# Spreading the group norm's factors over the partitions: a DRAM round trip replaced by products with the identity

## The chip, the core and the metric

The kernel runs on one core of a Trainium2 chip. TensorE multiplies matrices, VectorE, ScalarE and GpSimd work elementwise, SyncE issues transfers. On-chip data lie in 128 partitions (SBUF, and PSUM for the results of TensorE). The metric is device time in microseconds (us) of one execution, smaller is better.

## The reference

One inference step of a one-layer decoder, for 512 prompt tokens and 8 sample tokens, all in fp32. The part that matters here is the retention branch: 4 heads, 256 key and 512 value dimensions, each head with a root-mean-square group norm over its 512 values per token:

```python
o_r, s_new = retention(qr, kr, vr, s0, chunk)
o_r = o_r * lax.rsqrt(jnp.mean(o_r * o_r, axis=-1, keepdims=True) + EPS)
o_r = o_r.reshape(B, T, RET_V) * ret_gn_g.astype(f32) * jax.nn.silu(g_r.astype(f32))
branch_a = o_r.astype(xn.dtype) @ w_pa
```

Before it stand an RMS norm and one large input projection; beside it a dilated-window attention branch; behind it gates, an output projection and a SwiGLU feed forward.

## The kernel before

Activations are kept transposed, features on the partitions and the 520 tokens along the row, as two halves of 260 (256 prompt and 4 sample tokens). All weights are one stream of 194 tiles of 128x1024. Each tile is loaded by SyncE (`load_sub`), its high part is made by ScalarE and its low part by VectorE (`split_sub`, L153 and L157), two tiles ahead of use. `unit` is one 128-row block of a projection: 8 K-steps of 6 matmuls each (`product`, L189), into one of two PSUM product banks (`pm`), then an evacuation on VectorE or ScalarE.

All other work of TensorE is slipped between those K-steps. It is written as Python generators on two tracks, P and S. `pump` is called after each K-step and takes one step of one track; during retention P and S take turns, so a P step comes every second K-step. `drain` and `finish` take the remaining steps of a track at once, with no product between. `later(n, fn)` puts an operation n pumps further on. The order so written is the order of instructions on each engine; every engine takes its own instructions in order and waits for the others by semaphores.

For each of the four heads `h`: four units of q and k with the rotation (`rot`), four of v (`ev_v`, L621 and L622, which copies the sample tokens' values to `vs`), four of the gate (`ev_g`). On track P run `gen_scores`, `gen_vT` and then `gen_out`; on track S runs `gen_sample`, the recurrence of the sample tokens with its own small norm (L563 to L580; `os` is its row of results, and L570 its product of squares). A new head's `gen_out` is pushed after the old one has been finished by force. After the last head come six units of gates (`gate`, L659), then `drain()`, then the attention part, whose projections are evacuated by ScalarE (L849, L851) and VectorE (`sT`, L853).

`gen_out` computes the head's outputs into `GT` (16 tiles, four a head) and their squares' sum `acc` over four tiles. It then sums over the partitions with TensorE: 4 products with a column of ones (L468) give `sp`, 128 partitions by 4 columns, so token 128 j + p stands on partition p in column j. `rstd_rows` makes the factors `r` of them: one VectorE operation (L219) and a power on GpSimd (L221). To multiply `GT`, whose partitions are features, each factor is needed on all partitions as a row `rs` of 512 tokens. The kernel gets it by a store of `r` to the DRAM tile `rd[h]` (L473) and a load of it that is broadcast over the partitions (L474), both on SyncE's queue. Four yields later it multiplies: per tile one VectorE operation (L479), a yield, one GpSimd operation with the gate (L481), a yield.

`bcast_cols` (L224 to L228) is there already for the first and the second norm: for each column j a product whose weight is the column `r[:, j]` repeated 128 times and whose moving operand is the identity, so that every output partition holds the column as a row. Side results stand in PSUM banks from `sbank`, three in rotation.

Of the kernel before, what the change touches and what calls it, by code (L numbers as in the profile page):

```python
# [8 lines left out]
F32 = mybir.dt.float32  # L9
F32R = mybir.dt.float32r  # L10
AF = mybir.ActivationFunctionType
# [6 lines left out]
T, NS, C, D = 512, 8, 520, 1024  # L18
HF, HT = 260, 256
RH, DK, DV = 4, 256, 512  # L20
# [8 lines left out]
def tile_hybrid_layer(  # L29
# [9 lines left out]
    V, A, G_, PE, SP = nc.vector, nc.scalar, nc.gpsimd, nc.tensor, nc.sync  # L39
# [4 lines left out]
    dpool = ctx.enter_context(tc.tile_pool(name="dpool", bufs=1, space=DRAM))  # L44
# [4 lines left out]
    def open_pool(name, side):  # L49
        return tc.alloc_tile_pool(name=name, bufs=1, side=side, reuse_waits="tile")  # L50

# [1 line left out]
    def halves(ap):  # L53
        return ap.rearrange("p (f c) -> p f c", f=2)

    def tokv(ap):
        return halves(ap)[:, :, :HT]
# [7 lines left out]
    def f32(ap):  # L65
        return ap.bitcast(F32)

# [1 line left out]
    rp = open_pool("rp", "right")  # L69
    vec = cpool.tile([128, 40], F32, name="vec")  # L70
    warm = cpool.tile([128, 1], F32, name="warm")
# [14 lines left out]
    mhalf = cst[:, 273:274]  # L86
    g1v, g2v, gfv, gnv = vec[:, 0:8], vec[:, 8:16], vec[:, 16:24], vec[:, 24:40]

# [1 line left out]
    tracks = {"P": deque(), "S": deque()}  # L90
    pattern = ["P"]
    tick = [0]
# [2 lines left out]
    def later(n, fn):  # L95
        delayed.append([n, fn])
# [37 lines left out]
            run_delayed()  # L134
            step(name)

# [1 line left out]
    raw, split = {}, {}  # L138

    NRAW = 4  # L140
# [64 lines left out]
    def sbank(name="sp"):  # L205
        return pside.tile([128, 512], F32, tag="s", name=name)
# [7 lines left out]
    BL = 65  # L214

    def rstd_rows(pool, ssq, rows, ncol, n, tag):
        """(ssq / n + eps) ** -0.5 of the [rows, ncol] sums in ssq"""
        v = pool.tile([128, 8], F32, tag=tag + "v", bufs=2, name="v")
        V.tensor_scalar(v[:rows, :ncol], ssq, 1.0 / n, EPS, op0=ALU.mult, op1=ALU.add)  # L219
        r = pool.tile([128, 8], F32, tag=tag + "r", bufs=2, name="r")  # L220
        G_.tensor_tensor(r[:rows, :ncol], v[:rows, :ncol], mhalf[:rows].to_broadcast([rows, ncol]), op=ALU.pow)  # L221
        return r

    def bcast_cols(out, r, rows, ncol):  # L224
        """out[:, j, :rows] = r[:, j] as a row, on all partitions"""
        for j in range(ncol):
            PE.matmul(out[:, j, :], r[:rows, j:j + 1].to_broadcast([rows, 128]), ident[:rows, :rows],
                      start=True, stop=True)  # L228

# [1 line left out]
    X0 = bpool.tile([128, 16, C], F32R, tag="bg", name="X0")  # L231
    X = bpool.tile([128, 16, C], F32R, tag="bx", name="X")

    def tmp(name="t"):
        return rp.tile([128, C], F32, tag="t", bufs=6, name=name)

    sp = sbank("warmup")
# [92 lines left out]
    def xsrc(k):  # L330
        return X[:, k, :], X[:, 8 + k, :]

    # ================= retention =================
    SCO = (0, 512, 896, 1152)
    scs = [rp.tile([128, 1408], F32R, name=f"sc{i}") for i in range(2)]
    for i in range(2):
        G_.memset(f32(scs[i][:, 1152:1280]), 0.0)
    rd = [dpool.tile([1, T], F32, name=f"rd{h}") for h in range(RH)]
    vd = [dpool.tile([8, DV], F32, name=f"vd{h}") for h in range(RH)]

    for h in range(RH):
# [91 lines left out]
        def gen_out(h, tens):  # L433
            v, kt = tens["v"], tens["kt"]
            three = ((0, 0), (0, 1), (1, 0))
            acc = rp.tile([128, T], F32, tag="rs", name="ssa")
            for c in range(4):
                sp = sbank()
                for jb in range(4):
                    i0 = min(jb * 128, HT)  # L440
                    for x, y in three:
                        PE.matmul(sp[:, i0:], v[x][:, jb, c * 128:(c + 1) * 128], scs[y][:, SCO[jb]:SCO[jb] + T - i0],  # L442
                                  start=jb == 0 and x == y, stop=jb == 3 and x == 1)
                    if jb == 0:
                        yield
                yield
                A.activation(tokv(GT[:, 4 * h + c, :]), halves(sp), AF.Copy)
                if c == 0:
                    A.activation(acc, sp, AF.Square)
                else:  # L450
                    sq = tmp("sq")
                    A.activation(sq[:, :T], sp, AF.Square)
                    later(2, lambda sq=sq: G_.tensor_tensor(acc, acc, sq[:, :T], op=ALU.add))
            for dt in range(2):
                sp = sbank()
                for jb in range(4):
                    for x, y in three:
                        PE.matmul(sp, kt[x][:, jb, dt * 128:(dt + 1) * 128], v[y][:, jb, :], start=jb == 0 and x == y,  # L458
                                  stop=jb == 3 and x == 1)
                    if jb % 2:  # L460
                        yield
                sf = tmp("sf")
                A.activation(sf[:, :DV], sp, AF.Copy)
                yield
                later(2, lambda sf=sf, dt=dt: SP.dma_start(s_p[0, 0, h, dt * 128:(dt + 1) * 128, :], sf[:, :DV]))
            sp = sbank()
            for j in range(4):
                PE.matmul(sp[:, j:j + 1], acc[:, j * 128:(j + 1) * 128], ones1, start=True, stop=True)  # L468
            yield
            r = rstd_rows(rp, sp[:, :4], 128, 4, DV, "gn")  # L470
            rs = rp.tile([128, T], F32, tag="rs", name="rs")
            yield
            SP.dma_start(rd[h].rearrange("o (j p) -> p (o j)", p=128), r[:, :4])  # L473
            SP.dma_start(rs, rd[h].to_broadcast([128, T]))  # L474
            for _ in range(4):
                yield
            for c in range(4):
                o = tokv(GT[:, 4 * h + c, :])
                V.scalar_tensor_tensor(o, o, gnv[:, 4 * h + c:4 * h + c + 1], halves(rs), op0=ALU.mult, op1=ALU.mult)  # L479
                yield  # L480
                G_.tensor_tensor(o, o, tokv(tens["g"][:, c, :]), op=ALU.mult)  # L481
                yield
# [146 lines left out]
        if h == 0:  # L629
            GT = bpool.tile([128, 16, C], F32, tag="bg", name="GT")  # L630
        go = push("P", gen_out(h, tens))
        if h:
            finish("S", gs)
# [8 lines left out]
            unit(8, xsrc, ev_g)  # L642


    # ================= gates of the first half =================
    sgp = [None, None]
    SG = {}
    GC = ((0, 1, 2), (3, 4, 5, 6, 7))
# [1 line left out]
    def open_gates(i):  # L650
        sgp[i] = open_pool(f"sg{i}", "left")
        n = len(GC[i])
        t = sgp[i].tile([128, 2 * n, C], F32, name=f"SG{i}")
        for j, c in enumerate(GC[i]):
            SG[0, c], SG[1, c] = t[:, j, :], t[:, n + j, :]
# [11 lines left out]
    drain()  # L667
    rp.release()

    # ================= attention =================  # L670
    olp = open_pool("olp", "left")
    OT = olp.tile([128, 2, AH, C], F32R, name="OT")
    sT = olp.tile([128, 3, 3, 128], F32, name="sT")
# [188 lines left out]
    for g in range(3):  # L862
        push("S", gen_srow(g))

    # ================= gates of the second half =================
    open_gates(1)
    todo = [(c, w) for c in GC[1] for w in range(2)]
    for c, w in todo[:-2]:
# [19 lines left out]
        gate(c, w)  # L888
    drain()

    # ================= sample attention =================
    def gen_satt(sa):
        Pm = sa.tile([128, 3, 1024], F32, name="Pm")
        G_.memset(Pm, 0.0)
# [95 lines left out]
            V.tensor_tensor(OT[:, 1, :, f * HF + HT:(f + 1) * HF], sv[:, :, 4 * f:4 * f + 4], f32(hi), op=ALU.subtract)  # L990
        yield

    # ================= merge =================
    GB = bpool.tile([128, 16, C], F32R, tag="bx", name="GB")
    for k in range(8, 16):
        gsplit(k, GB, 2 * k - 16)
# [22 lines left out]
    olp.release()  # L1019
    sgp[0].release()  # L1020

    # ================= output projection, residual, second norm =================
    hp = open_pool("hp", "left")
    hT = hp.tile([128, 8, C], F32, name="hT")
    rs2 = hp.tile([128, C], F32, name="rs2")
# [32 lines left out]
    def gen_norm2():  # L1058
        for _ in range(8):
            yield  # L1060
        sp = sbank()
        for j in range(8):
            PE.matmul(sp[:BL, j:j + 1], acc2[:, BL * j:BL * j + BL], ones1, start=True, stop=True)
        yield
        r = rstd_rows(fp, sp[:BL, :8], BL, 8, D, "n2")
        yield
        yield
        yield
        for f in range(2):
            sp = sbank()  # L1070
            bcast_cols(sp[:, :HF].rearrange("p (j c) -> p j c", c=BL), r[:, 4 * f:4 * f + 4], BL, 4)
            V.tensor_copy(rs2[:, f * HF:(f + 1) * HF], sp[:, :HF])
            yield

    # ================= feed forward =================
    pattern[:] = ["P"]
    push("P", gen_norm2())
    U = [None] * (2 * NFF)
# [34 lines left out]
    def fin_T(c, f):  # L1113
        h = hT[:, c, :]
        sp, sp2 = sbank(), sbank()
        for j in range(2):
            o = f * HF + 128 * j
            pe_T(sp[:, j * 128:(j + 1) * 128], h[:, o:o + 128])
        pe_T(sp2[:4, :128], h[:, f * HF + HT:(f + 1) * HF])
        return sp, sp2  # L1120
# [62 lines left out]
    for f in range(2):  # L1183
        pm = pmain.tile([128, 2, 512], F32, tag="pm", name="pm")
        for k in range(NFF):
# [3 lines left out]
            if f == 1 and k == 2:  # L1189
                a = fin_T(7, 0)  # L1190
# [3 lines left out]
    a = fin_T(7, 1)  # L1194
# [35 lines left out]


def _tiles(w):
    """[K, N] -> [N/128 column tiles][K/128][128, 128]"""
    k, n = w.shape
    return w.reshape(k // 128, 128, n // 128, 128).transpose(2, 0, 1, 3)

# [45 lines left out]
```

## Time and profile before

| | us |
|---|---|
| three runs, median (lowest to highest) | 1393.46 (1391.36 to 1395.12) |
| profiled execution: span from first to last instruction | 1389.1 |
| TensorE busy (matmul) in that span | 1310.0 |
| VectorE, ScalarE, GpSimd busy | 671.7, 479.9, 111.0 |

The three runs are other executions than the profiled one, whose own time outside the span is not listed. Engines in the profile: PE is TensorE's matmul, PEld its weight load, DVE VectorE, ACT ScalarE, POOL GpSimd, SPq SyncE's queue. L479 is line 479 of the kernel before. A timeline row gives start, duration, engine, line, operation, output<-inputs, shapes, count and, in brackets, the idle time of the engine ahead of it with what ended it. A row of a windows view gives the window, its length, the busy time and count of PE, PEld, DVE, ACT and POOL, then the clock granted to TensorE, the share of DMA time and GB/s.

### The profile page before, as it was taken

How to read it: one execution, taken by the hardware profiler on the slowest of the kernel's cores; microseconds unless marked ns; L12 is line 12 of the kernel's file. 1: busy time of each engine (PE TensorE's matmuls, PEld its weight loads, DVE VectorE, ACT ScalarE, POOL GpSimd, SP SyncE). 2: the span in 40 equal slices, each digit the busy share in tenths (PEclk: the TensorE clock that was granted, in tenths of full speed). 3: DMA queues.
4: the chain of work that ended last, by engine and by line, in shares of the span. 5: the costliest groups of instructions: out<-in, count | busy, mean ns of one | idle time of the engine just before them, and what ended most of it. 6: DMA issues, size and time to landing. Idle time of an engine off the chain costs nothing.

```text
span 1389.1 us, 25071 instructions
## 1 busy us (share of the span) xinstructions
PE 1310.0 (94%) x10640; PEld 1280.2 (92%) x10640; DVE 671.7 (48%) x1256; ACT 479.9 (35%) x835; POOL 111.0 (8%) x84
## 2 busy tenths in 40 slices
PE   8999899899899799999999967699999999999997
PEld 8999899899799799999999966599999999999997
DVE  7856565574563433443434633346544444443333
ACT  4554263363264144333333410123322222222222
POOL 3601201202201100000000000011000000000000
PEclk9999999999999899999999988899999999999999
DMA  6285375384473234343334466734333332233321
GB/s 236 67 276 172 89 264 180 119 269 144 136 248 126 76 95 115 97 119 88 108 107 120 137 192 179 237 109 136 109 91 92 93 92 92 92 100 98 92 62 62
DMA packets 94432, 184.51 MB, mean 133 GB/s; under 512 B 14344, under 2 KB 36552, under 8 KB 94320
## 3 DMA queue, kind: packets, MB, share of 16 engines
q1 hardware_dynamic: 93600, 181.85, 42.2%
q8 instruction: 83, 1.36, 0.4%
q10 hardware_dynamic: 720, 1.07, 0.2%
q14 instruction: 29, 0.24, 0.1%
HBM read 156.75 MB, written 26.13 MB: 132 GB/s over the span
## 4 chain that ended last, share of the span: by engine, by line
PE 74%; DMA 12%; DVE 6%; issue 3%; SPq 2%; POOL 1%; ACT 1%; DVEq 0%; ACTq 0%; POOLq 0%
PE pm L189 65%; DMA area<-qd 5%; DMA rd<-r 3%; PE sp L442 2%; PE sp L212 2%; DVE wl L157 1%; SPq L920 1%; DMA rs<-rd 1%; PE sp L458 1%; PE sp L762 1%; DVE GT L479 1%; PE sp L394 1%; DMA vb<-vd 1%; DMA cb<-cd 1%; PE sp L712 1%
## 5 line engine op out<-in xcount | busy, mean ns | idle before, releaser
L189 PE MATMUL pm<-X,wh 128*128 128x260 f32 x4608 | 757.9, 287 | 20.1 <-DVE sT L853 10.0
L189 PEld LDWEIGHTS pm<-X,wh 128*128 128x128 f32 x4608 | 639.2, 190 | 32.4 <-DVE sT L853 10.2
L189 PE MATMUL pm<-X,wl 128*128 128x260 f32 x2304 | 466.2, 284 | 0.0
L189 PEld LDWEIGHTS pm<-X,wl 128*128 128x128 f32 x2304 | 357.6, 190 | 0.2 <-DVE wl L254 0.2
L157 DVE TENSOR_TENSOR wl<-raw,wh 128x1024 fp32r<-128x1024 f32 x192 | 240.2, 1252 | 137.1 <-ACT wh L153 136.6
L153 ACT ACTIVATE wh<-raw 128x1024 fp32r<-128x1024 f32 x192 | 201.7, 1051 | 229.5 <-PE pm L189 181.0
L189 PE MATMUL pm<-UB,wh 128*128 128x260 f32 x448 | 85.3, 282 | 0.0
L189 PEld LDWEIGHTS pm<-UB,wh 128*128 128x128 f32 x448 | 67.2, 188 | 0.0
L545 DVE SCALAR_TENSOR_TENSOR st<-st,kv 128x512 f32<-128x512 f32 x64 | 48.6, 774 | 22.6 <-ACT kv L510 19.7
L221 POOL TENSOR_TENSOR r<-v,cst 128x4 f32<-128x4 f32 (+4 forms) x14 | 17.7, 1273 | 517.4 <-DVE v L219 517.2
L189 PE MATMUL pm<-UA,wh 128*128 128x260 f32 x256 | 55.3, 287 | 0.0
L189 PE MATMUL pm<-UA,wl 128*128 128x260 f32 x256 | 54.1, 283 | 0.0
L931 DVE SCALAR_TENSOR_TENSOR area<-area 128x128 f32<-128x128 f32 x96 | 22.4, 289 | 64.5 <-DMA area<-qd 64.3
L853 DVE TENSOR_SCALAR sT<-pm 128x8 f32<-128x8 f32 x36 | 6.0, 166 | 96.0 <-ACT vT L851 23.6
L510 ACT ACTIVATE kv<-vb,ks 128x512 f32<-128x512 f32 x64 | 44.1, 718 | 22.9 <-DMA vb<-vd 22.6
L189 PE MATMUL pm<-GA,wh 128*128 128x260 f32 x256 | 44.7, 300 | 3.4 <-DVE SG L1003 3.4
L189 PE MATMUL pm<-GB,wh 128*128 128x260 f32 x256 | 45.1, 302 | 0.0
L189 PEld LDWEIGHTS pm<-GA,wh 128*128 128x128 f32 x256 | 37.7, 202 | 4.8 <-issue 4.8
L1089 ACT ACTIVATE fa<-fa 128x520 f32<-128x520 f32 x22 | 14.0, 638 | 78.3 <-DVE fa L1088 78.3
L189 PE MATMUL pm<-M,wh 128*128 128x260 f32 x256 | 41.1, 282 | 0.0
L189 PEld LDWEIGHTS pm<-UA,wh 128*128 128x128 f32 x256 | 40.4, 188 | 0.4
L189 PEld LDWEIGHTS pm<-UA,wl 128*128 128x128 f32 x256 | 40.5, 188 | 0.0
(244 smaller groups left out, 1457.3 us busy)
## 6 DMA issues: line engine op xcount, KB each, us to landing
raw<-wall SPq DMA_DIRECT2D x192, 512.0 KB
st<-state SPq DMA_DIRECT2D x64, 256.0 KB
out<-st SPq DMA_DIRECT2D x64, 256.0 KB
area<-ck SPq DMA_DIRECT2D x24, 512.0 KB
vb<-vd SPq DMA_DIRECT2D x32, 256.0 KB
area<-qd SPq DMA_DIRECT2D x24, 256.0 KB
cb<-cd SPq DMA_DIRECT2D x4, 768.0 KB
xr<-xT SPq DMA_DIRECT2D x8, 260.0 KB
```

Source lines behind the costliest of these rows:

```text
L153: A.activation(h, r, AF.Copy)
L157: V.tensor_tensor(l, r, f32(h), op=ALU.subtract)
L189: PE.matmul(pm[:, f, :HF], w, x[:, f * HF:(f + 1) * HF], start=first, stop=last)
L212: PE.transpose(out, in_, ident[:n, :n])
L221: G_.tensor_tensor(r[:rows, :ncol], v[:rows, :ncol], mhalf[:rows].to_broadcast([rows, ncol]), op=ALU.pow)
L394: PE.matmul(sp[:, :T - i0], x[:, dt, jb * 128:(jb + 1) * 128], y[:, dt, i0:], start=i == 0, stop=i == len(mm) - 1)
L442: PE.matmul(sp[:, i0:], v[x][:, jb, c * 128:(c + 1) * 128], scs[y][:, SCO[jb]:SCO[jb] + T - i0], start=jb == 0 and x == y, stop=jb == 3 an ...
L458: PE.matmul(sp, kt[x][:, jb, dt * 128:(dt + 1) * 128], v[y][:, jb, :], start=jb == 0 and x == y, stop=jb == 3 and x == 1)
L510: A.activation(kvs[i][:, :DV], vbs[b], AF.Copy, scale=ks[:, dt, b:b + 1])
L545: V.scalar_tensor_tensor(sts[i], sts[i], GAMMA[h], kvs.pop(i)[:, :DV], op0=ALU.mult, op1=ALU.add)
L931: V.scalar_tensor_tensor(pr[:, u, e], kvbuf(i)[:, u, e], 1.0, qbuf(i)[:, u, e], op0=ALU.mult, op1=ALU.mult, accum_out=S[:, g, 32 * h + b + ...
L1089: A.activation(t, t, AF.Silu)
```

## The change

In `gen_out` the DRAM tiles, the store and the load are taken out. The factors `r` are spread by `bcast_cols` into a PSUM bank and copied by ScalarE to `rs`. The four yields that stood behind the load now stand ahead of the spreading; a yield lies between spreading and copy, and one between copy and multiplications. The other lines of the diff take out comments and docstrings, and are not shown.

```diff
-    rd = [dpool.tile([1, T], F32, name=f"rd{h}") for h in range(RH)]
     vd = [dpool.tile([8, DV], F32, name=f"vd{h}") for h in range(RH)]
...
             r = rstd_rows(rp, sp[:, :4], 128, 4, DV, "gn")
             rs = rp.tile([128, T], F32, tag="rs", name="rs")
-            yield
-            SP.dma_start(rd[h].rearrange("o (j p) -> p (o j)", p=128), r[:, :4])
-            SP.dma_start(rs, rd[h].to_broadcast([128, T]))
             for _ in range(4):
                 yield
+            sp = sbank()
+            bcast_cols(sp.rearrange("p (j c) -> p j c", c=128), r[:, :4], 128, 4)
+            yield
+            A.activation(rs, sp, AF.Copy)
+            yield
             for c in range(4):
                 o = tokv(GT[:, 4 * h + c, :])
                 V.scalar_tensor_tensor(o, o, gnv[:, 4 * h + c:4 * h + c + 1], halves(rs), op0=ALU.mult, op1=ALU.mult)
                 yield
                 G_.tensor_tensor(o, o, tokv(tens["g"][:, c, :]), op=ALU.mult)
                 yield
```

## The prediction

> **What bounds the kernel now.** I read the page first, then the time that TensorE waited up to 480 us (the retention part, where all the changed lines lie), then the same view for VectorE and for SyncE's queue.
>
> ```profile
> span 1389.1 us, 25071 instructions
> PE 1310.0 (94%) x10640; PEld 1280.2 (92%) x10640; DVE 671.7 (48%) x1256; ACT 479.9 (35%) x835; POOL 111.0 (8%) x84
> ...
> PE pm L189 <- DVE sT L853: 10.0, 1, 10.0
> PE sp L570 <- DVE os L567: 6.0, 1, 6.0
> PE pm L189 <- DVE vs L622: 5.0, 2, 2.7
> ...
> PE sp L212 <- DVE vs L622: 2.9, 2, 1.7
> ...
> PE sp L394 <- DVE ph L382: 1.0, 1, 1.0
> ...
> PE sp L394 <- DVE pl L382: 0.6, 1, 0.6
> ...
> DVE GT L479 <- DMA rs<-rd: 38.2, 4, 10.6
> ...
> SPq L474 <- DMA rd<-r: 38.2, 4, 11.9
> ...
> rs<-rd SPq DMA_DIRECT2D x4, 256.0 KB
> ...
> rd<-r SPq DMA_DIRECT2D x4, 2.0 KB
> ```
>
> TensorE works 94% of the span, so the kernel is bound by its instructions plus the gaps between them. The columns of the wait rows are total, count and longest. The six rows of TensorE add up to 10.0 + 6.0 + 5.0 + 2.9 + 1.0 + 0.6 = 25.5 us, and all name VectorE. VectorE itself waited 38.2 us in four pieces, one per head, for the factors `rs`; SyncE's queue waited as long for the store `rd` to land before it could issue the load. The last two rows are those transfers, 2 KB out and 256 KB in per head. To see that these are the same events I read the timeline around the first and the last head.
>
> ```profile
> 129.60 1.03 POOL L221 TENSOR_TENSOR r<-v,cst 128x4 f32<-128x4 f32 x1 [18.11 <-DVE v L219]
> ...
> 130.66 0.39 SPq L473 DMA_DIRECT2D rd<-r  x1
> ...
> 131.84 1.07 PE L555 MATMUL oacc<-y,om 128*32 128x512 f32 x8
> ...
> 140.35 0.34 SPq L474 DMA_DIRECT2D rs<-rd  x1
> ...
> 144.60 0.75 DVE L479 SCALAR_TENSOR_TENSOR GT<-GT,vec,rs 128x512 f32<-128x512 f32 x1 [9.49 <-DMA rs<-rd]
> 145.27 0.18 DVE L566 COPY os<-sp 128x32 f32<-128x32 f32 x1
> ...
> 145.74 0.63 PE L570 MATMUL sp<-os,cst 128*128 128x32 f32 x2 [5.99 <-DVE os L567]
> ```
>
> In the first head the factor `r` is ready at 130.63. The 2 KB store is issued at 130.66, the load only at 140.35 (9.69 us later), and the first multiplication on VectorE starts at 144.60. VectorE takes its instructions in order, so the copy `os` (L566) stood behind that multiplication: it followed at once, at 145.27, and TensorE had stood 5.99 us for it.
>
> ```profile
> 444.90 2.62 POOL L221 TENSOR_TENSOR r<-v,cst 128x8 f32<-128x8 f32 x2 [16.19 <-DVE v L219]
> ...
> 448.56 0.61 ACT L659 ACTIVATE SG<-pm 128x520 f32<-128x520 f32 x1 [4.82 <-PE pm L189]
> ...
> 460.10 0.60 ACT L849 ACTIVATE kT<-pm 128x512 f32<-128x512 f32 x1 [4.22 <-PE pm L189]
> 460.19 4.75 DVE L479 SCALAR_TENSOR_TENSOR GT<-GT,vec,rs 128x512 f32<-128x512 f32 x4 [10.56 <-DMA rs<-rd]
> ...
> 469.86 0.15 DVE L853 TENSOR_SCALAR sT<-pm 128x8 f32<-128x8 f32 x1
> ...
> 470.06 1.24 PE L189 MATMUL pm<-X,wh 128*128 128x260 f32 x4 [10.00 <-DVE sT L853]
> ```
>
> In the last head the track is drained after the last gate, whose product ends near 448.5. VectorE waits until 460.19 for `rs`, then has 9.67 us of queued work before it evacuates a product (L853, 469.86). TensorE has two product banks: it filled them by 460.1 and stood 10.0 us.
>
> **What goes, part by part.** The removal of the DRAM trip lets VectorE start its multiplications as soon as TensorE and ScalarE have spread the factors. The 25.5 us above are the first term. A second is the clock after three of the gaps.
>
> ```profile
> 145.74:151.53 5.79, 5.79 (x26) 5.79 (x27) 4.56 (x6) 0.00 (x0) 5.06 (x3) 0.50 0.29 90
> ...
> 357.70:360.41 2.71, 0.00 (x1) 0.00 (x1) 0.88 (x3) 2.67 (x4) 0.05 (x1) 0.93 0.80 252
> 360.41:363.18 2.77, 2.77 (x13) 2.70 (x14) 2.77 (x3) 0.77 (x1) 2.77 (x2) 0.50 0.03 6
> ...
> 470.06:476.44 6.38, 6.38 (x30) 6.38 (x31) 2.29 (x3) 0.00 (x0) 0.00 (x0) 0.53 0.71 246
> ...
> 147.63 1.07 PE L189 MATMUL pm<-X,wh 128*128 128x260 f32 x4
> ...
> 148.93 1.07 PE L189 MATMUL pm<-X,wh 128*128 128x260 f32 x4
> ...
> 152.38 0.64 PE L189 MATMUL pm<-X,wh 128*128 128x260 f32 x4
> ...
> 153.10 0.64 PE L189 MATMUL pm<-X,wh 128*128 128x260 f32 x4
> ```
>
> The third column from the right of a window is the granted clock. Behind the gaps of heads 0, 2 and 3 it is 0.50, 0.50 and 0.53. One K-step of six matmuls then takes 148.93 - 147.63 = 1.30 us, against 153.10 - 152.38 = 0.72 us, so 45% of the slow time is lost: 0.45 x 5.79 = 2.6, 0.45 x 2.77 = 1.2, and for the last (five steps in 6.38 us) 6.38 - 5 x 0.72 = 2.8. Together 6.6 us. Gaps and slow clock make 32.1 us.
>
> [...]
>
> **What comes in.** Per head, four fp32 products of a 128x128 weight (a factor column repeated) with the 128-column identity. The nearest row is the attention product of the same shape, which is in the trace as two instructions per product:
>
> ```profile
> 496.73 1.56 PE sp L762 x14
> ...
> L463 ACT ACTIVATE sf<-sp 128x512 f32<-128x512 f32 x8 | 4.7, 589 | 11.4 <-PE sp L458 11.4
> ...
> L468 PE MATMUL sp<-cst,ssa x32: 164/250/250, 124.4 to 444.6; 128*128 128x1 f32 x32
> ```
>
> 14 instructions take 1.56 us, 0.111 us each; a head adds 8 of them, 0.89 us, four heads 3.6 us. This lies fully on the path, since TensorE is the bound. The bounds are zero (if all fell into gaps that remain) and twice that (a clock at half rate), 7.1 us; I take 3.6 because at full rate the row has the same shape.
>
> ScalarE gets one copy of 128x512 out of PSUM per head, 0.59 us by the second row. ScalarE is 35% busy and mostly waits for TensorE, so this is nothing in itself; the weight split `wh` queued behind it is late by at most that, and it is made two stream tiles ahead of its use. Without that lead it would be 4 x 0.59 = 2.4 us. The two DMAs per head leave SyncE's queue, where the weight loads stood behind them. That can only bring loads forward, and TensorE has no wait for a weight load among the rows above, so I count nothing for it.
>
> The multiplications come one step of the primary track later than before (six yields after `rstd_rows` where there were five). A track step is every second K-step, about 1.44 us. The forced finish before the next head's outputs takes up the extra step, so I count nothing for that.
>
> **New waits.** Three: TensorE's spreading waits for `r` from GpSimd, with all following products queued behind it; ScalarE's copy waits for TensorE, with weight splits and evacuations behind it; VectorE's multiplication waits for that copy, with `os`, `vs`, `sT` and the low weight parts behind it. In the first head the sums (L468) start at 124.4. The spreading stands five track steps, ten K-steps, later: 124.4 + 0.9 (eight instructions) + 10 x 0.72 + 1.07 for the L555 group on the way = 133.6, about 3.0 us after `r` is ready. In the last head the two `r` end at 447.52 and the drain puts the spreading directly behind the last gate, near 448.5: 1.0 us of margin. So TensorE should not wait for `r`.
>
> What is late next: in the last head, spreading to 449.4, copy to about 450.2 (the gate's evacuation at 448.56 is ahead of it, perhaps a 1.05 us weight split too), then the same 9.67 us of VectorE work, so L853 at 459.9 to 461.0, with TensorE ready for it at 460.07 + 0.9 = 461.0. The gap shrinks from 10.0 to between 0 and 1, with the signals on the way. In heads 1 and 2 VectorE no longer has a backlog when `vs` arrives, but a low weight part can stand in front, up to about 1 us each; head 0 the same. I leave 2 us in the sum (0 to 4 as bounds).
>
> **Sum.** -25.5 - 6.6 + 3.6 + 2.0 = -26.5 us. Nothing later gives it back: after 480 us the work starts when TensorE gets there. The profiled span becomes 1389.1 - 26.5 = 1362.6. The profile lists the span and not that execution's own time; the span lies 4.4 us under the median run of 1393.46 (three runs, 1391.36 to 1395.12), and I take those 4.4 us to stay: 1367.0 us.
>
> **Rivals.**
>
> *VectorE's queue becomes the wait (chance 0.13).* The DRAM trip was also time in which nothing else was asked of VectorE. If the multiplications, slowed while GpSimd multiplies beside them (four took 4.75 us at 460.19 against 0.75 us for the one at 144.60), still hold `vs` and `sT` back about 3 us per head and the clock drops behind one such gap (2.8 us), 12 + 2.8 - 2 = 12.8 us of the gain go: 1379.8 us. For it speaks that in the last head I find almost no slack; against it, that VectorE idled 38.2 us in these stretches.
>
> *The trip is hidden anyway (0.03).* If the TensorE gaps would come in any case, by another late operation, only the 3.6 us of new products would be left: 1397.1 us, within 0.3% (4.2 us, about what a measurement of this kernel can tell from no change). Against it: in head 0 `os` had only that one multiplication ahead of it. [...]
>
> *TensorE waits for GpSimd (0.03), the side of slower.* TensorE now stands in order behind `r`. To come out over 0.3% slower the waits must eat 32.1 - 3.6 + 4.2 = 32.7 us, 8.2 us a head, which needs `r` some 11 us later in head 0 than it was (3.0 us margin), 9 us later in the last. The time would be 1398 or more. GpSimd is 8% busy and had sat idle 18.11 us before the first `r`, 16.19 us before the last, so this decides only if GpSimd's multiplications of one head ran into the next head's `r`; they end well before.
>
> **How the numbers follow.** The forecast has 0.81. Its own range is the sum without remaining waits and without the cost of the products (32.1 us off: 1361.4) to products at 7.1 and waits at 4 (21.0 off: 1372.5). The first rival has to be reached into, to 1379. With one microsecond for the spread of a run the range is 1360 to 1379. Faster by over 0.3%: 0.94 (forecast and first rival); within: 0.03; slower: 0.03.
>
> **What would show it.** Right: VectorE's wait for `rs` from DMA is gone and the wait for ScalarE's copy is under 1 us a head; TensorE's rows for L570, L622 and L853 drop below 1 us each; the granted clock stays at 1.0 between 130 and 480 us; L227 has 32 more instructions of about 0.11 us start to start. Wrong: a row of TensorE waiting for GpSimd's L221, a gap before the third attention product that is still over 3 us, or weight loads that land later than before.

## The result and the profile after

The changed kernel takes 1372.72 us (median of four runs, 1370.15 to 1376.72), the kernel before beside it 1394.29 us (1391.36 to 1395.82): a ratio of 0.985, 95% interval 0.982 to 0.988, or 21.6 us less. A second chip gave 1370.82 against 1386.4 us, 0.988 (0.986 to 0.991). The forecast was 1367.0 and 26.5 us less. One execution of one experiment, 3258.84 us, was slow from end to end; nothing is read from its trace and its time is left out.

The page of the changed kernel, then the waits of TensorE and (in the stretch of the first head) of VectorE:

```profile
span 1369.2 us, 25133 instructions
## 1 busy us (share of the span) xinstructions
PE 1313.0 (96%) x10672; PEld 1284.1 (94%) x10672; DVE 665.5 (49%) x1256; ACT 481.7 (35%) x839; POOL 104.5 (8%) x84
```
```profile
PE sp L393 <- DVE ph L381: 0.9, 1, 0.9
PE sp L393 <- DVE pl L381: 0.8, 2, 0.6
```
```profile
DVE GT L480 <- ACT rs L476: 0.3, 1, 0.3
```

The gaps of TensorE behind L570, L622 and L853 are gone from the list. What is left of the six rows is 1.7 us before the scores (L393, where it was L394). These two waits were there before, with 1.0 and 0.6 us, so the change did not touch them; the other four rows, 23.9 us, are gone whole. VectorE's wait for the factors, 38.2 us in four pieces, is down to a few tenths in a head. The timeline of the first and of the last head shows the chain that took its place:

```profile
130.49 1.03 POOL L221 TENSOR_TENSOR r<-v,cst 128x4 f32<-128x4 f32 x1 [18.01 <-DVE v L219]
...
134.66 1.05 PE L227 MATMUL sp<-cst,r 128*128 128x128 f32 x8
135.74 0.60 ACT L476 ACTIVATE rs<-sp 128x512 f32<-128x512 f32 x1 [3.41 <-PE sp L227]
136.38 0.75 DVE L480 SCALAR_TENSOR_TENSOR GT<-GT,vec,rs 128x512 f32<-128x512 f32 x1 [0.27 <-ACT rs L476]
...
430.64 2.62 POOL L221 TENSOR_TENSOR r<-v,cst 128x8 f32<-128x8 f32 x2 [16.24 <-DVE v L219]
...
434.11 1.05 PE L227 MATMUL sp<-cst,r 128*128 128x128 f32 x8
...
435.26 0.60 ACT L476 ACTIVATE rs<-sp 128x512 f32<-128x512 f32 x1 [0.35 <-PE sp L227]
...
435.89 4.82 DVE L480 SCALAR_TENSOR_TENSOR GT<-GT,vec,rs 128x512 f32<-128x512 f32 x4 [0.51 <-ACT rs L476]
```

From `r` (131.52) to the first multiplication are 4.9 us, most of it the yields that the code puts there; before it was 14.0. TensorE reaches the spreading 3.1 us after `r` in the first head and 0.85 us after it (433.26) in the last, and waits in neither.

**Where the rest went.** Two landmarks are the same instructions in both kernels: ScalarE's first `kT` in the second group of the attention, and TensorE's first value product of the sample attention (`sacc`). In the rows below they are the first of the two times. The kernel before, then the changed one:

```profile
L851 ACT ACTIVATE kT<-pm x8: 598/599/600, 492.8 to 705.5; 128x512 f32<-128x512 f32 x8
...
L972 PE MATMUL sacc<-area,Pm x192: 272/273/297, 895.0 to 916.0; 128*32 128x128 f32 x192
```
```profile
L852 ACT ACTIVATE kT<-pm x8: 598/599/600, 466.5 to 679.1; 128x512 f32<-128x512 f32 x8
...
L973 PE MATMUL sacc<-area,Pm x192: 272/273/297, 875.0 to 896.1; 128*32 128x128 f32 x192
```

The changed kernel is 26.3 us ahead at the first landmark, within 0.2 of the forecast sum, and only 20.0 ahead at the second. So 6.3 us were given back in between, in a stage that the change does not touch. From the last gate (ScalarE's `SG`, 772.9 and 746.6) to `sacc` it lasts 122.1 us before and 128.4 after. In it the rows of q, stored to the DRAM tiles `qd` beforehand, are loaded again, broadcast over the partitions. VectorE waits for these loads for more than half of the stage, before and after (the first number is the total), and SyncE's queue issues the 24 of them from 779.6 to 862.6 before and from 753.2 to 845.3 after (the last two numbers of a row are the first and the last start):

```profile
DVE area L931 <- DMA area<-qd: 64.3, 22, 6.8
L920 SPq DMA_DIRECT2D area<-qd x24: 465/2096/5065, 779.6 to 862.6; - x24
```
```profile
DVE area L932 <- DMA area<-qd: 71.0, 23, 9.2
L921 SPq DMA_DIRECT2D area<-qd x24: 462/2724/5064, 753.2 to 845.3; - x24
```

83.0 us became 92.1, and VectorE's wait for them 71.0 us instead of 64.3. The median issue went from 2096 to 2724 ns, which alone proves little: other traces with `qd` at its old place have medians up to 2671 ns. What can have changed for the loads? Not their number, size or order. But without the `rd` tiles the DRAM tiles made later move down: by the addresses in the two built programs `qd` stood at offsets 212992, 278528 and 344064 and now stands 16 KB lower. That, and a mere spread from run to run, were the two theories for this part.

### The profile page after: what moved, and what is told of

The parts are those of the page before. It is cut to its first block, busy times and chain, and to the rows that moved or that the text cites. A ratio compares the mean times of both kernels' runs of the same rounds, so it can differ in the third digit from the quotient of the medians.

```text
span 1369.2 us, 25133 instructions
## 1 busy us (share of the span) xinstructions
PE 1313.0 (96%) x10672; PEld 1284.1 (94%) x10672; DVE 665.5 (49%) x1256; ACT 481.7 (35%) x839; POOL 104.5 (8%) x84
## 3 DMA queue, kind: packets, MB, share of 16 engines
q10 hardware_dynamic: 720, 1.07, 0.2%
## 4 chain that ended last, share of the span: by engine, by line
PE 85%; DMA 7%; SPq 3%; DVE 3%; ACT 1%; POOL 1%; issue 1%; DVEq 0%; ACTq 0%
PE pm L189 73%; DMA area<-qd 5%; PE sp L212 2%; PE sp L441 2%; PE sp L457 2%; SPq L921 1%; PE sp L393 1%; PE sp L763 1%; SPq L913 1%; DMA cb<-cd 1%; PE oacc L556 1%; DVE wl L157 1%; PE sp L713 1%; PE sp L227 1%; PE sacc L973 1%
## 5 line engine op out<-in xcount | busy, mean ns | idle before, releaser
L189 PE MATMUL pm<-X,wh 128*128 128x260 f32 x4608 | 755.0, 286 | 5.1 <-DVE X L244 3.3
L189 PEld LDWEIGHTS pm<-X,wh 128*128 128x128 f32 x4608 | 636.1, 189 | 17.1 <-issue 6.7
L189 PE MATMUL pm<-X,wl 128*128 128x260 f32 x2304 | 464.7, 283 | 0.0
L189 PEld LDWEIGHTS pm<-X,wl 128*128 128x128 f32 x2304 | 356.3, 189 | 0.1
L189 PE MATMUL pm<-UB,wh 128*128 128x260 f32 x448 | 85.3, 282 | 0.0
L189 PEld LDWEIGHTS pm<-UB,wh 128*128 128x128 f32 x448 | 67.2, 188 | 0.0
L546 DVE SCALAR_TENSOR_TENSOR st<-st,kv 128x512 f32<-128x512 f32 x64 | 45.6, 723 | 23.2 <-ACT kv L511 20.9
L189 PE MATMUL pm<-GA,wh 128*128 128x260 f32 x256 | 47.5, 313 | 9.1 <-DVE SG L1004 9.1
L189 PE MATMUL pm<-UA,wh 128*128 128x260 f32 x256 | 55.3, 287 | 0.0
L189 PE MATMUL pm<-UA,wl 128*128 128x260 f32 x256 | 54.1, 283 | 0.0
L189 PEld LDWEIGHTS pm<-GA,wh 128*128 128x128 f32 x256 | 40.4, 216 | 11.0 <-issue 11.0
L189 PE MATMUL pm<-GB,wh 128*128 128x260 f32 x256 | 45.0, 301 | 0.0
L189 PE MATMUL pm<-M,wh 128*128 128x260 f32 x256 | 41.1, 282 | 0.0
L189 PEld LDWEIGHTS pm<-UA,wh 128*128 128x128 f32 x256 | 40.4, 188 | 0.3
L189 PE MATMUL pm<-GB,wl 128*128 128x260 f32 x128 | 28.0, 302 | 13.2 <-DVE wl L157 13.0
```

Of the source, the lines that this page charges most:

```text
L189: PE.matmul(pm[:, f, :HF], w, x[:, f * HF:(f + 1) * HF], start=first, stop=last)
L546: V.scalar_tensor_tensor(sts[i], sts[i], GAMMA[h], kvs.pop(i)[:, :DV], op0=ALU.mult, op1=ALU.add)
```

## The experiments

Two questions: was VectorE's order the cause of the gaps, or SyncE's queue, held up by the store; and what took 6 us back? In the texts on record "the landmark in the attention" is the `kT` start above (they call it the third product of the second group; it is the second, k). Their figures for the loads of q count from the first cache load, 0.4 us sooner than those told here, and the first of them count a shorter piece of the stage: 106.7 and 113.1 us of the 122.1 and 128.4.

**Both kernels once more, unaltered.**

> The changed kernel once more, unaltered, for its time and a second trace. In the first trace it was 26.3 us ahead when the second set of gates ended, and only 20.0 us ahead after the sample attention: that stage, from the first of its loads' buffers being free to its score products, took 113.1 us against 106.7 before. Theory 'spread of that stage from run to run': here the stage lies somewhere between 105 and 115 us, and the ratio to the kernel before is 0.981 to 0.986. Theory 'the change lengthens that stage': about 113 us again.

> The kernel before once more, unaltered, for a second trace. Theory 'spread from run to run': its sample attention stage need not be 106.7 us again, it may be 104 to 114. Theory 'the change lengthens that stage': 106 to 107 us. The gaps of TensorE in the retention part stay as they were: 25.5 us within 1.

The changed kernel: 0.988 (0.986 to 0.991), stage 130.9 us, loads of q issued over 93.7 us. The kernel before: stage 120.5 us, 82.7 us. Each came back to its own side, which speaks against mere spread. The gaps of the kernel before were there again (9.8 us behind `sT`, 6.2 behind `os`), but the six rows add up to 23.4 us, just outside the 25.5 within 1 that I expected. The landmarks stood at 465.7 and 488.3, the second 4.5 us sooner than in the first trace of that kernel.

**The DRAM tiles of the attention part back at their old offsets.** The store that fills the enlarged tile still writes its first 8 rows.

```diff
-    vd = [dpool.tile([8, DV], F32, name=f"vd{h}") for h in range(RH)]
+    vd = [dpool.tile([8 if h else 16, DV], F32, name=f"vd{h}") for h in range(RH)]
...
-            SP.dma_start(vd[h], vrow[:NS, :DV])
+            SP.dma_start(vd[h][:8, :], vrow[:NS, :DV])
```

> The changed kernel, with one DRAM tile 16 KB larger (the rows are not used), so that the DRAM tiles of the attention part stand at the offsets that they had before the change; no instruction is added. Theory 'the DRAM offsets set how long the broadcast loads of the sample attention take': the stage goes back to about 107 us, and the kernel to about 1366 to 1368 us, 5 below the changed kernel. Theory 'spread from run to run': the same time as the changed kernel within 0.3%, and a stage anywhere between 104 and 115.

1363.58 us (1361.8 to 1364.56), where the changed kernel on the same chip had 1370.82 (1367.3 to 1375.43): the ranges don't meet, and the difference is 7.2 us where I expected 5. The ratio to the kernel before is 0.982 (0.980 to 0.985). The stage lasts 121.3 us. Here 16 KB of unused DRAM gave back what the stage had taken.

```profile
L921 SPq DMA_DIRECT2D area<-qd x24: 463/2224/4533, 753.9 to 837.6; - x24
```

**Only the qd tiles at their old offset**, twice: once for its time, once for its trace. The store and the load of `cd` still use its first 3 * T elements (not shown).

```diff
-    cd = [dpool.tile([1, 3 * T], F32, name=f"cd{h}") for h in range(AH)]
+    cd = [dpool.tile([1, 3 * T + (4096 if h == 3 else 0)], F32, name=f"cd{h}") for h in range(AH)]
```

> The changed kernel, with the last of the cd tiles 16 KB larger (unused), so that of all DRAM tiles only the three qd tiles, which the sample attention's broadcast loads read, stand where they stood before the change. In the traces so far the broadcast loads are issued over 83.5 and 83.1 us (kernel before), 92.5 and 94.1 (changed kernel), 84.1 and 82.0 (the two with the old offsets). Theory 'the offset of qd decides': 82 to 85 us again and a time 5 to 9 us below the changed kernel, about 0.982 of the kernel before. Rival 'another tile's offset, or the spread': 91 to 95 us, and 0.986 to 0.989.

> The changed kernel with the qd tiles at their old offset once more, for its trace: the first trace of this kernel was taken of a single disturbed execution of 3258.84 us. Theory 'the offset of qd decides': broadcast loads issued over 82 to 85 us, attention landmark at 465 to 468 us, span 1358 to 1364. Rival: over 90 us, span 1368 or more.

Ratio 0.983 (0.981 to 0.985), runs of 1362.19 to 1365.23 us. The trace has 86.6 us for the loads of q and a stage of 124.7: most of the way back, a little above the range that I gave, and the span of 1364.8 is 0.8 over it.

```profile
L921 SPq DMA_DIRECT2D area<-qd x24: 462/2496/5332, 752.6 to 839.2; - x24
```

**The kernel before, with qd moved the other way.** The same edit with 12288 for 4096 puts `qd` at offset 262144.

> The kernel before, with the last cd tile 48 KB larger (unused), which moves the qd tiles from offset 212992 to 262144. So far the broadcast loads of q are issued over 82.0 to 84.1 us at 212992 (five traces), 92.5 and 94.1 at 196608, 90.3 at 200704. Theory 'where the qd tiles stand decides, and a multiple of 64 KB (196608 is one, 262144 too) is a bad place': 90 to 95 us and a kernel 7 to 11 us slower than before. Rival 'only that one place is bad': 82 to 85 us and the time of the kernel before. Rival 'not the place at all': either.

1396.44 us against 1386.1, ratio 1.007 (1.006 to 1.009): a kernel whose instructions are those of the kernel before is 10.3 us slower because one tile stands elsewhere. The traced execution (1391.64 us, the shortest of the six) shows 88.6 us for the loads and a stage of 125.3.

```profile
L920 SPq DMA_DIRECT2D area<-qd x24: 462/2441/5284, 777.0 to 865.6; - x24
```

The time came as the first theory expected it, the loads 1.4 us short of its range. So in these kernels the place decides. Which property of it does is open: 196608 gave 92.1, 93.4 and 93.7, 262144 gave 88.6, but 200704, no multiple of 64 KB (an experiment below), gave 90.3 too, and only 212992 gave 81.6 to 86.6 (six traces).

**The DRAM trip issued beside the products.**

```diff
+    rd = [dpool.tile([1, T], F32, name=f"rd{h}") for h in range(RH)]
...
+            yield
+            dummy = rp.tile([128, T], F32, tag="dummy", name="dummy")
+            SP.dma_start(rd[h].rearrange("o (j p) -> p (o j)", p=128), r[:, :4])
+            SP.dma_start(dummy, rd[h].to_broadcast([128, T]))
-            for _ in range(4):
+            for _ in range(3):
                 yield
```

> The changed kernel, and beside it the store of the factors and the broadcast load are still issued on SyncE's queue where they were before, into a tile that nothing reads. So SyncE's queue is held up as before, and VectorE is not. Theory 'VectorE's order was the cause' (mine): TensorE's gaps in the retention part stay below 3 us, and the time is that of the changed kernel within 0.4%. Rival 'SyncE's queue was the cause': the weight and state loads come late again, TensorE's gaps come back, and most of the 21 us are lost (1385 to 1394).

```profile
SPq L475 <- DMA rd<-r: 34.6, 4, 9.7
PE sp L394 <- DVE ph L382: 0.9, 1, 0.9
PE sp L394 <- DVE pl L382: 0.8, 2, 0.6
```

SyncE's queue stood 34.6 us for the store, where it had stood 38.2 in the kernel before, and TensorE's waits were those of the changed kernel; the landmark came at 466.5. So the queue was not the cause. The time, 1360.43 us, is 10.4 below the changed kernel on the same chip, and not equal to it as I expected. The reason is the place of `qd`: with the `rd` tiles in use all DRAM tiles stand where they did before (stage 117.8 us, loads 81.6). Against the kernel with the tiles moved back (1361.8 to 1364.56) its runs are 1358.4 to 1362.26; why they lie a little lower was not followed.

**The multiplications ten yields after the load instead of four**, in the kernel before.

> The kernel before, with the multiplications ten yields behind the load instead of four: no products, SyncE's queue is held as before, only VectorE comes to its wait later. Theory 'VectorE's order' (mine): the gaps of heads 0 and 1 go (6.0 and about 4 us and the slow clock of 2.6), since ten yields are about 14 us and the trip took 13.9; in head 2 and in the last head the track is drained before the load has landed, so most of 5.5 and the 10.0 stay. The attention's first landmark (third product of the second group) comes at 474 to 482 us, against 492.8 and 488.3 before and 466.5 changed. Rival 'SyncE's queue': no change, 488 to 493.

A miss, and the most instructive one. VectorE waited 2.1 us for `rs` in the first three heads together, the gaps behind `os` and `vs` were gone, and yet the landmark came at 492.0. TensorE's waits in this kernel:

```profile
PE pm L189 <- DVE sT L853: 10.6, 1, 10.6
PE sp L394 <- DVE ph L382: 10.5, 2, 5.8
```
```profile
262.61 2.28 DVE L382 TENSOR_TENSOR ph<-qT,ph 128x1024 fp32r<-128x1024 f32 x1
264.81 1.21 DVE L382 TENSOR_TENSOR pl<-kT,pl 128x1024 fp32r<-128x1024 f32 x1
264.94 0.79 PE L394 MATMUL sp<-ph,pl 128*128 128x512 f32 x1 [4.72 <-DVE ph L382]
```

The later multiplications now ran into the forced finish before the next head's outputs. They came in one bunch, beside GpSimd's, and the low parts for the next head's scores (L382), behind them, came late: a new wait of 4.7 and 5.8 us, with the slow clock behind it (0.50 from 264 to 268 us; four matmuls of L189 took 1.07 us at 267.95 and 0.64 at 271.09). The first rival of the prediction would have struck on the same queue, though at `vs` and `sT`. The schedule had room for a shorter trip, not for a later use.

**The trip in the last head alone.** (`if h == 3:` the old lines, else the new ones.)

> The changed kernel, with the DRAM trip back in the last head alone. By my sum that head is worth 10.0 us of gap and 2.8 of slow clock less 0.9 for the products: the landmark in the attention comes 11.9 us later than in the changed kernel, at 477 to 479 us against 465.7 to 468.1. If the gain came from heads 0 to 2 in the main, under 8 us. Its qd tiles stand 4 KB from where the changed kernel has them; I have no forecast for the broadcast loads (82 to 95 us).

The landmark came at 479.0 us, 10.9 to 13.3 us behind those of the changed kernel and its variants with other offsets (465.7 to 468.1); TensorE's gap behind `sT` was 11.0, against 10.0 in the kernel before. The term of the last head stands: 11.9 us were expected.

**The products twice over.**

```diff
-            bcast_cols(sp.rearrange("p (j c) -> p j c", c=128), r[:, :4], 128, 4)
+            for _ in range(2):
+                bcast_cols(sp.rearrange("p (j c) -> p j c", c=128), r[:, :4], 128, 4)
```

> The changed kernel with each head's four spreading products done twice over (the same result written twice), to price them. Theory: 8 instructions at 0.111 us more per head, on the path: the landmark in the attention 3.6 us later than in the changed kernel, at 469.3 to 471.7 against 465.7 to 468.1. Rival 'they fall into gaps': no later.

469.7 us, 1.6 to 4.0 later than in the kernels with one set, and 3.2 and 4.0 later than in the two traces of the changed kernel itself. In this one trace the products do lie on the path, and the price of 3.6 us stands within the spread. (Its loads of q, at the changed kernel's offset, were issued over 93.4 us.)

**The same step in the sample attention.** If broadcast loads of q bound that stage, they can be replaced as those of the factors were: a column of the identity, repeated, picks one row of q and puts it on all partitions.

```diff
-                    SP.dma_start(qbuf(i)[:, u, :].rearrange("p (h e) -> p h e", h=4), src)
...
+        def spreadq(i, u):
+            g, b = work[i]
+            sp = sbank()
+            for h in range(AH):
+                m = 32 * h + b + u
+                PE.matmul(sp[:, h * 128:(h + 1) * 128], ident[:, m:m + 1].to_broadcast([128, 128]), qrow[:, g, :],
+                          start=True, stop=True)
+            return sp
```

> The changed kernel, and the same step taken once more in the sample attention: the rows of q are spread over the partitions by products with a column of the identity, into PSUM, and VectorE reads them there; the 24 broadcast loads of 256 KB are gone. 96 products of two instructions at 0.111 us are 21 us of TensorE, in a stage where it idles about 35 us. Theory 'that stage is bound by its broadcast loads': the stage from the last gate to the value products falls from 121 to 131 us to about 95 to 105 (TensorE's own work of about 86 us and the 21), and the kernel is 15 to 30 us below the changed one. Rival 'the cache loads bound it alike': less than 8 us.

1336.63 us (1335.28 to 1338.88), ratio 0.964 (0.962 to 0.966): the fastest kernel of the study, 50 us below the kernel before and, by the ratios, 29 to 34 below the changed one, where I expected 15 to 30. The windows view of the stage, the changed kernel first; the columns are the window, its length, busy time and count of PE, PEld, DVE, ACT and POOL, the granted clock, the DMA share and GB/s:

```profile
746.60:875.00 128.40, 90.89 (x624) 87.80 (x622) 49.08 (x238) 18.88 (x24) 0.00 (x0) 0.83 0.65 182
```
```profile
745.80:841.70 95.90, 95.90 (x816) 95.79 (x814) 48.35 (x238) 19.04 (x24) 0.00 (x0) 1.00 0.50 173
```

TensorE, with 192 instructions more, is busy for the whole stage at the full clock. It no longer depends on those loads, and not on where `qd` stood.

**The change measured without them.** The same edit in the kernel before.

> The kernel before with q of the sample attention spread on the chip, and the group norm's factors still by DRAM. It differs from the last faster kernel (ratio 0.9639 to the kernel before) only in the change that was predicted, and neither reads a qd tile. Theory 'the change is worth about 26 us wherever the broadcast loads of q don't depend on where their tile stands': 26 us slower than that kernel, ratio 0.980 to 0.984 to the kernel before, and the attention landmark at 488 to 493 us. Rival 'the change is worth the 20 us that the first comparison showed': ratio 0.976 to 0.979.

1363.94 us, ratio 0.984 (0.982 to 0.986), and 0.964 with the change: 2.0% of the kernel before, or 27.9 us, with an uncertainty of about 4 us from the two intervals. The traces put the landmarks at 490.1 and 466.0 and the spans at 1359.0 and 1335.7: 24.1 and 23.3 us, so here next to nothing is given back.

## Why the prediction was right, point by point

The direction and the mechanism of the gain held, and the time lies in the range (1372.72 in 1360 to 1379). The forecast was 5.7 us too far down, or 4.9 us in the gain. That the range held is in part luck: by its own terms, products and remaining waits, it ended at 1372.5. What carried it further was one microsecond of spread and a rival that did not come true, and what used up the room was an effect that the prediction did not think of.

*The gaps.* The wait in VectorE's order was the cause: shown by the trip beside, where SyncE's queue was held and TensorE was not. 25.5 us of gaps became 1.7. Two errors cancel in this: the 1.6 us before the scores were counted among what goes, and stayed; the 2.0 us left in the sum for waits at `vs` and `sT` did not come.

*The slow clock.* 6.6 us were expected to go. One slow window stayed, where the remaining 1.7 us fall:

```profile
354.00:362.00 8.00, 6.60 (x32) 6.12 (x33) 5.30 (x8) 2.07 (x3) 0.00 (x0) 0.79 0.67 203
```

A mean of 0.79 in 8 us, with 0.50 in the slow part, is 8 x 0.21 / 0.5 = 3.4 us of slow clock, 1.5 us lost at the prediction's 45%. So remaining waits and slow clock cost 3.2 us in this trace, where 2.0 were put in, and the sign that the clock stays at 1.0 failed. But the same waits (0.94 and 0.64 us) left the clock alone in the second trace of the changed kernel, in the same window:

```profile
354.00:362.00 8.00, 6.42 (x44) 5.83 (x44) 5.71 (x8) 2.08 (x3) 0.00 (x0) 1.00 0.62 195
```

The term of 1.2 us behind the gap of head 2 is as unsteady: from 340 to 372 us the granted clock was 0.95 in the first trace of the kernel before and 1.00 in the second, behind a gap of 2.57 us where the first had 2.71.

*The products.* 3.6 us forecast; doubling them moved the landmark by 3.2 and 4.0 against the two traces of the changed kernel.

*Sum at the landmark.* -26.3 us in the first pair of traces. Over all traces in which the factors go by DRAM as before, the landmark scatters from 488.3 to 492.8 (four, mean 490.5), and over those in which they go by one set of products in all heads, from 465.7 to 468.1 (six, mean 466.6): 23.9 us on average against 26.5. So the 0.2 us by which the first pair met the forecast is luck too.

*The step that failed* is "Nothing later gives it back: after 480 us the work starts when TensorE gets there." It does start then, but the sample attention lasted 6 to 10 us longer, because the removal of the `rd` tiles moved the `qd` tiles. The removal of the DRAM tiles was not priced at all, and it weighed about as much as the whole term of the slow clock (6.6 us). That the place of the `qd` tiles is the cause is shown in both directions; why one place is worse is not.

*The rivals.* TensorE never waited for GpSimd, with the margins of 3.1 and 0.85 us that the prediction had at 3.0 and 1.0. The trip was not hidden: in head 0 of the kernel before, the load was issued 9.69 us after the store, and VectorE's multiplication started another 4.25 us later. VectorE's queue did not become the wait in the change itself, but in the kernel before it did, at the low parts for the scores, as soon as the multiplications were put later.

## What to carry to other kernels

The round trip of 2 KB through DRAM cost here what stood behind its consumer in program order (in head 0 TensorE's 6.0 us for `os`), not what the consumer did with the factors (0.75 us for that multiplication); look for the first instruction of another chain behind the one that waits. When the trip is removed, measure by landmarks, stage by stage: a stage that the diff doesn't touch can take part of the gain back (here 6.3 of 26.3 us), and then the layout of what the diff removed is among the suspects. And where one broadcast through DRAM was on the path, look for the next: taking out the one in the sample attention was worth 22 us in the kernel before (1386.1 to 1363.94) and 29 to 34 in the changed one, about as much as the change that was predicted.

## What the runs showed of the hardware

The time of broadcast loads depended on where their 64 KB sources stood in DRAM: 24 loads were issued over 81.6 to 86.6 us at offset 212992 (six traces) and over 88.6 to 93.7 us at 196608, 200704 and 262144 (five traces), and 10.3 us of a kernel's time hung on it (1396.44 against 1386.1). With rows picked by a column of the identity in their place, TensorE had no gap left in the stage (busy 95.90 of 95.90 us, against 90.89 of 128.40), and the granted clock there was 1.00 against 0.83. So an estimated 21 us more of TensorE's work (192 instructions at 0.111 us) went with a stage that was 32.5 us shorter. A short wait did not always cost the clock: waits of 0.94 and 0.64 us were followed by an estimated 3.4 us at half clock in one execution of the changed kernel (a mean of 0.79 from 354 to 362 us) and by none in another (1.00).
